# Seven products for keys and a quarter of the queries, and a plain projection stage in source order

## The chip, the core and the metric

The kernel runs on one NeuronCore of one Trainium2 chip. The metric is the device time of one execution in microseconds; the kernel before takes 2573.16 us (median of 3 runs, 2572.2 to 2574.59). Five engines work side by side, each through its own instructions in order: TensorE (PE in the profile) multiplies, VectorE (DVE) and ScalarE (ACT) do elementwise work, GpSimd (POOL) does some of it and issues some transfers, SyncE (SP) only issues transfers; ACT issues transfers too.

## What is computed

One layer of an encoder over 768 tokens (512 of a prompt, 256 of a sample), in float32:

```python
def hybrid_layer(x, ...):
    h = rmsnorm(x, ln_mix_g)
    z = h @ w_in                      # 2048 -> 2560: fourier 1024 | q 1024 | k 256 | v 256
    of = fourier_mix(zf, w_fourier)   # per 128-channel group: Re(2-D DFT), then a linear map
    q = apply_rope(q, cos, sin)
    k = apply_rope(k, cos, sin)
    oa = window_attention(q, k, v, attn_sink)
    mixed = concatenate([rmsnorm(of, ...), rmsnorm(oa, ...)])
    x = x + mixed @ w_out
    h = rmsnorm(x, ln_mlp_g)
    u = relu(h @ w_up)                # 2048 -> 8192
    return x + (u * u) @ w_down
```

A final rmsnorm follows. In the softmax a learned number per head ("sink") stands in the denominator.

## The kernel before

**Arithmetic.** Every large product is made of three TensorE products of split operands: `split` writes a rounded part with ACT ("high", `wh`) and the remainder with DVE ("low", `wl`), and high*high, high*low and low*high are added in PSUM. A TensorE instruction here multiplies a 128x128 block of weights by 384 tokens (half of them, `HALF`) or by 512 columns.

**Seven products.** Where 2x2 blocks allow it, eight block products are replaced by seven (Winograd's form of Strassen's scheme): the four blocks of weights and of tokens are added and subtracted, and the seven results are added. The MLP uses it throughout (lines 1229 and 1664), and so does the Fourier quarter of `w_in`.

**Order of the first stages.** (1) Until 41 us: the tokens are loaded, scaled and split, and `v` is computed. (2) The seven-product stage for the 1024 Fourier columns: `names7` names the products in order (a11, s1, s2, s3, a22, s4, a12). `cols7` does not exist yet: the columns come in 2 groups `g` of two 256-column blocks, and each product has 2 halves `e` of the sum, so there are 4 steps to a product and `NP7` = 28 steps. Step `n` calls, in this order: `sum7(n+3)` (DVE adds weight blocks), `high7(n+3)` (ACT), `low7(n+2)` (DVE), the token sums and splits that are due (`high_at` on ACT, `low_at` on DVE), `product7(n)` (24 TensorE instructions), `out7(n-1)` (copies a result from PSUM by ACT, or adds it to an earlier one by DVE; finished results are stored by ACT's queue), `load7(n+5)` (SP). SP, ACT, DVE and PE take these in source order. The norms of the rows are taken on the way: `row_load` (POOL's queue) and `row_square` (ACT) in four rounds at steps 10 to 18, then `row_norms` (DVE and POOL), `row_turn` (a transpose on PE after step 21) and `row_spread`.
(3) The plain stage: 20 pieces (5 blocks of 256 columns: k and four of q; 4 pieces to a block, 48 TensorE instructions each, line 835). `piece_split(p+2)` splits the weights two pieces ahead and calls `piece_load(p+4)`. Between the halves of the pieces stands the Fourier work of eight groups (`fold`, `stage1`, `stage2`; `after(t, fn)` puts `fn` behind piece `t`, where x.5 is the middle), and from piece 10 on the rotation of k and of three blocks of q (`cross` on POOL, `turned` on DVE, `parts` on ACT and DVE, stores by ACT's queue). Here only PE is in source order (SP for the first loads, and all engines from piece 19 on); for the others a planner chooses the order.
(4) Attention and the output projection, by a list of due times (`at`, `later`); the last block of q is rotated there. (5) The MLP.

PSUM has eight banks. In the seven-product stage before, four carry the tag `f` and four the tag `ps`; results of s1 and s4 get banks of their own (`Y`).

## Time and profile before

| what | value |
|---|---|
| median of 3 runs | 2573.16 us |
| the profiled execution | 2573.4 us, its span 2571.6 us |
| granted TensorE clock | 0.999 |
| MLP, share of the chain that ended last | line 1229 36%, line 1664 35% |
| output projection, the same (line 1082) | 10% |
| plain stage, the same (line 835) | 5% |
| seven products of `w_in`, the same (line 277) | 5% |

The share of a line in the chain is the part of the span in which the work that ended last went through that line. Time is taken off by shortening a stage only if its own bound is shortened: where PE is always busy, PE instructions.

### The profile page before, as it was taken

Reading aid. Unit: us, or ns where it says so; the run is one execution under the profiler, and the core shown is the slowest. Engines: PE = TensorE matmul, PEld = TensorE weight load, DVE = VectorE, ACT = ScalarE, POOL = GpSimd, SP = SyncE. Lnnn points to the kernel's source line nnn. Section 1 sums busy time; section 2 is a strip of 40 time slices with the busy share of each in tenths; the row PEclk is TensorE's granted clock in tenths of the full one; section 3 lists DMA queues with packets and bytes.
Section 4 is the critical chain, followed back from the end, with each engine's and each line's share of the span. In section 5 each row is a group of like instructions: output and inputs, shape, how many; then the busy total and the mean of one; then the engine's idle time right before and its main releaser. Section 6 shows DMA issues by size and latency. Waiting matters only on the chain.

```text
span 2571.6 us, 34801 instructions
## 1 busy us (share of the span) xinstructions
PE 2561.1 (100%) x13463; PEld 2345.3 (91%) x13463; DVE 1793.4 (70%) x2221; ACT 1121.7 (44%) x1622; POOL 242.9 (9%) x345
## 2 busy tenths in 40 slices
PE   9999999999999999999999999999999999999998
PEld 9999998888899999999999999988888888888887
DVE  8966468786465565656777777667766766777687
ACT  7644337674233333334445444433333333333335
POOL 0102322223201001100000000100000000000000
PEclk9999999999999999999999999999999999999999
DMA  8753567455655454456666666775543662554364
GB/s 305 234 182 122 178 186 207 142 165 191 222 178 181 154 174 168 164 190 239 218 227 230 213 217 214 266 285 176 175 154 121 216 227 85 175 185 158 101 210 153
DMA packets 259671, 487.84 MB, mean 190 GB/s; under 512 B 20586, under 2 KB 147056, under 8 KB 259248
## 3 DMA queue, kind: packets, MB, share of 16 engines
q1 hardware_dynamic: 187968, 321.77, 39.4%
q10 hardware_dynamic: 58512, 112.05, 11.5%
q0 software_dynamic: 13024, 51.79, 6.1%
q8 instruction: 106, 1.74, 0.3%
q14 instruction: 61, 0.50, 0.1%
HBM read 365.99 MB, written 119.54 MB: 189 GB/s over the span
## 4 chain that ended last, share of the span: by engine, by line
PE 97%; DVE 1%; DMA 1%; issue 0%; POOL 0%; SPq 0%; ACT 0%; POOLq 0%; DVEq 0%; ACTq 0%
PE pu L1229 36%; PE pd L1664 35%; PE pm L1082 10%; PE pz L835 5%; PE p L277 5%; PE pv L447 1%; PE o L960 1%; PE s L881 1%; PE t L938 1%; PE pe L664 0%; PE pa L643 0%; PE ptx L137 0%; DVE zs L729 0%; DMA raw<-in_w_out 0%; POOL zy L720 0%
## 5 line engine op out<-in xcount | busy, mean ns | idle before, releaser
L1229 PE MATMUL pu<-xf,wh 128*128 128x384 f32 x3072 | 780.2, 334 | 0.0
L1229 PEld LDWEIGHTS pu<-xf,wh 128*128 128x128 f32 x3072 | 554.2, 188 | 1.5 <-ACT o L1247 1.3
L1664 PE MATMUL pd<-wh,sh 128*128 128x512 f32 x1332 | 517.7, 389 | 0.0
L1664 PE MATMUL pd<-wl,sh 128*128 128x512 f32 x1332 | 517.7, 389 | 0.0
L1664 PE MATMUL pd<-wh,sl 128*128 128x512 f32 x1332 | 517.5, 389 | 0.0
L1229 PE MATMUL pu<-xf,wl 128*128 128x384 f32 x1536 | 513.1, 334 | 0.0
L1641 ACT ACTIVATE wh<-rd 128x1024 fp32r<-128x1024 f32 x200 | 202.3, 1054 | 522.3 <-PE pd L1664 422.0
L1651 DVE TENSOR_TENSOR wl<-rd,wh 128x1024 fp32r<-128x1024 f32 x200 | 236.0, 1221 | 226.4 <-ACT wh L1641 225.6
L1209 ACT ACTIVATE wh<-ur 128x1024 fp32r<-128x1024 f32 x160 | 170.1, 1063 | 382.6 <-PE pu L1229 207.9
L1664 PEld LDWEIGHTS pd<-wl,sh 128*128 128x128 f32 x1332 | 250.0, 188 | 51.9
L1664 PEld LDWEIGHTS pd<-wh,sl 128*128 128x128 f32 x1332 | 249.9, 188 | 52.0 <-DVE sl L1652 0.3
L1664 PEld LDWEIGHTS pd<-wh,sh 128*128 128x128 f32 x1332 | 250.0, 188 | 51.7
L1229 PEld LDWEIGHTS pu<-xf,wl 128*128 128x128 f32 x1536 | 288.3, 188 | 0.0
L1215 DVE TENSOR_TENSOR wl<-ur,wh 128x1024 fp32r<-128x1024 f32 x160 | 195.4, 1221 | 76.1 <-ACT wh L1209 76.1
L1250 DVE TENSOR_TENSOR o<-pu,o 128x768 f32<-128x768 f32 x160 | 152.8, 956 | 122.5 <-PE pu L1229 114.9
L1634 DVE TENSOR_TENSOR rd<-rd 128x1024 f32<-128x1024 f32 x112 | 131.7, 1217 | 0.0
L1229 PE MATMUL pu<-xs,wh 128*128 128x384 f32 x512 | 129.8, 334 | 0.0
L1209 ACT ACTIVATE wh<-sx 128x1024 fp32r<-128x1024 f32 x64 | 67.9, 1062 | 130.5 <-PE pu L1229 104.3
L277 PE MATMUL p<-xs,wh 128*128 128x384 f32 x448 | 113.7, 334 | 0.0
L1652 DVE TENSOR_TENSOR sl<-sr,sh 128x768 fp32r<-128x768 f32 x111 | 105.5, 951 | 0.0
L1215 DVE TENSOR_TENSOR wl<-sx,wh 128x1024 fp32r<-128x1024 f32 x64 | 78.2, 1222 | 23.8 <-ACT wh L1209 23.6
L1229 PEld LDWEIGHTS pu<-xs,wh 128*128 128x128 f32 x512 | 92.5, 188 | 0.0
(295 smaller groups left out, 3843.2 us busy)
## 6 DMA issues: line engine op xcount, KB each, us to landing
rd<-in_w_down SPq DMA_DIRECT2D x176, 512.0 KB, 5.2
ur<-in_w_up SPq DMA_DIRECT2D x128, 512.0 KB, 3.9
sr<-sd SPq DMA_DIRECT2D x95, 384.0 KB, 5.4
pd<-o ACTq DMA_DIRECT2D x60, 384.0 KB, 2.3
o<-pd POOLq DMA_DIRECT2D x60, 384.0 KB, 6.0
sd<-sm ACTq DMA_DIRECT2D x60, 384.0 KB, 2.8
raw<-in_w_in SPq DMA_DIRECT2D x39, 512.0 KB, 4.2
raw<-in_w_out SPq DMA_DIRECT2D x32, 512.0 KB, 4.7
```

The lines of the kernel that those rows point to most:

```text
L277: nc.tensor.matmul(ps7[bank, g, r][:, :HALF], l[:, i, r * P : (r + 1) * P], x[:, o, 4 * e + i, :], start=(opens and e == 0 and i == 0 and ...
L835: nc.tensor.matmul(ps[c][s][:, :HALF], w[:, i, cs], whole[j // 2][s][o][:, 4 * (j % 2) + i, :], start=first and n == 0, stop=stop and n == 2,)
L1082: nc.tensor.matmul(ps, l(k), w[:, k % 2, :], start=(k == 0 and n == 0), stop=(k == 7 and n == 2))
L1209: nc.scalar.activation(wh[:], raw[:], AF.Copy)
L1215: nc.vector.tensor_tensor(out=wl[:], in0=raw[:], in1=f32(wh[:]), op=ALU.subtract)
L1229: nc.tensor.matmul(ps[:, t, :HALF], w[:, i, t * P : (t + 1) * P], xb[:, o, i, :], start=(s == first_of[bank] and i == 0 and n == 0), stop= ...
L1250: nc.vector.tensor_tensor(out=o, in0=src, in1=o, op=ALU.add)
L1634: add = lambda x, y, op: nc.vector.tensor_tensor(out=x[:], in0=x[:], in1=y[:], op=op)
L1641: nc.scalar.activation(wh[:], t[:], AF.Copy)
L1651: nc.vector.tensor_tensor(out=wl[:], in0=t[:], in1=f32(wh[:]), op=ALU.subtract)
L1652: nc.vector.tensor_tensor(out=sl[:], in0=sr[:], in1=f32(sh[:]), op=ALU.subtract)
L1664: nc.tensor.matmul(o, l[:, q, ts], w[:, ns], start=(j == j0 and (q, t) == (0, 0)), stop=(j == j1 and (q, t) == (1, 2)),)
```

## The change

1. `cols7` adds a third group to the seven-product stage: block 6 (q columns 512 to 767 of q) and block 8 (k). 42 steps instead of 28. The plain stage keeps 12 pieces (q columns 0 to 255, 256 to 511 and 768 to 1023) instead of 20.
2. The PSUM banks of that stage are laid out anew (`pp0`): six banks `x` that every group keeps for the sums over a11, s2, s3 and a22, and two banks `t` for s1, s4 and a12, one for each row block `r`. The groups use these two in turn. `product7` finishes row block 0 before it begins row block 1, and `out7(n, 0)` empties block 0 in step `n`, `out7(n, 1)` block 1 in step `n+1`. The result of a11 is stored to DRAM and loaded again (`back7`) for the last sum.
3. The order in a step: `product7(n)`, `out7(n-1, 1)`, `low7(n+2)`, `out7(n, 0)`, `sum7(n+3)`, `high7(n+3)`, `high_at`, `low_at`, `k_at`, stores, `load7(n+5)`. The token steps are laid at other numbers, the row norms at steps 16 to 28.
4. k is rotated in steps 29 to 43 of that stage; the scaled tables of the rotation are stored and loaded again.
5. The plain stage is in source order on all engines from its first instruction; the Fourier groups begin one piece earlier and the rotations are laid at pieces 1 to 10.
6. In the softmax the sign of the queries and of the mask is turned, so that a minimum takes the place of a maximum and one small DVE instruction per head goes. The part of SBUF that is kept for the descriptors of POOL's transfers is 4096 instead of the default number of bytes.

```diff
+        pp = pctx.enter_context(tc.tile_pool(name="pp0", bufs=1, space=PSUM, reuse_waits="tile"))
-        NP7 = 4 * len(names7)
+        cols7 = ((0, 1), (2, 3), (6, 8))
+        NS7 = 2 * len(cols7)
+        NP7 = NS7 * len(names7)
...
         def product7(n):
+            name, g, e = of7(n)
+            own = name in ("s1", "s4", "a12")
+            opens = own or name == "a11"
             wh, wl = w7.pop(n)
-            x = xs[w % 2]
-            for i in range(4):
-                for r in range(2):
+            x = xs[n // NS7 % 2]
+            for r in range(2):
+                if e == 0 and opens:
+                    ps7[own, g, r] = pp.tile([P, 512], F32, tag="t" if own else "x", bufs=2 if own else 6, name="p7")
+                for i in range(4):
                     for q, (l, o) in enumerate(((wh, 0), (wh, 1), (wl, 0))):
...
+            elif s == "s4":
+                z, put = c7.pop((0, g, r)), (0, 1)
+                add(z, z)
+            else:
+                z, put = c7.pop((2, g, r)), (0, 0)
+                add(z, z)
+            if put:
+                c, t = put
+                dst = home7(g, c, r)[:, t * HALF : (t + 1) * HALF]
+                put7.append(lambda: nc.scalar.dma_start(dst, z[:]))
...
+            step(low_at, 12 + 2 * e, lambda e=e: difference(e))
+            step(high_at, 13 + 2 * e, lambda e=e: xhigh(h1, fx["d"], e))
+            step(low_at, 13 + 2 * e, lambda e=e: xlow(l1, fx["d"], h1, e))
+            step(low_at, 16 + e, lambda e=e: xsum(b11, b21, b11, e))
+            step(high_at, 18 + e, lambda e=e: xhigh(h0, b11, e))
+            step(low_at, 19 + e, lambda e=e: xlow(l0, b11, h0, e))
...
+            for s, n in enumerate((36, 38, 40)):
+                step(k_at, n - 1, lambda s=s: k_cross(s))
+                step(k_at, n, lambda s=s: k_turn(s))
+                step(k_at, n, lambda s=s, n=n: k_parts(s, n))
...
             for n in range(NP7):
+                product7(n)
+                out7(n - 1, 1)
+                low7(n + 2)
+                out7(n, 0)
+                sum7(n + 3)
+                high7(n + 3)
                 for fn in high_at.get(n, ()):
                     fn()
-                sum7(n + 3)
-                high7(n + 3)
-                low7(n + 2)
                 for fn in low_at.get(n, ()):
                     fn()
-                product7(n)
-                out7(n - 1)
+                for fn in k_at.get(n, ()):
+                    fn()
+                stores7(1 if n % 2 else 0)
                 load7(n + 5)
...
-                if n == 18:
+                if n == 24:
                     row_norms()
-                if n == 21:
+                if n == 26:
                     row_turn()
...
-            out7(NP7 - 1)
-            out7(-1)
+            out7(NP7 - 1, 1)
+            stores7()
+            for n in range(NP7, NP7 + 2):
+                for fn in k_at.get(n, ()):
+                    fn()
...
-        n_in = 4 * len(cols)
+        n_in = 4 * (len(cols) - 2)
...
-        with tc.manual_schedule(engines={mybir.EngineType.SP}):
-            piece_load(0)
-            piece_load(1)
+        last = ExitStack()
+        last.enter_context(tc.manual_schedule(engines={SP, Activation, DVE, Pool}))
+        piece_load(0)
+        nc.sync.dma_start(cc[:], a["c_chan"])
...
+        piece_load(1)
+        load_group(0)
+        open_rotation()
+        load_z(1)
+        load_group(1)
         piece_split(0)
         piece_split(1)
```

More of the change, by code (lines that the diff above doesn't have):

```diff
@@ new lines, in parts_of @@
+        def parts_of(z, hi, out, scale, s, when=lambda dt, fn: fn(), dts=(0, 0)):
+            ts = slice(s * 256, (s + 1) * 256)
+            put = lambda o, x: nc.scalar.dma_start(out[o][:, ts].rearrange("(b p) t -> p b t", p=P), x)
+            if scale is None:
+                nc.scalar.activation(hi, z, AF.Copy)
+                low = lambda: nc.vector.tensor_tensor(out=z.bitcast(F32R), in0=z, in1=f32(hi), op=ALU.subtract)
+            else:
+                nc.scalar.activation(hi, z, AF.Copy, scale=scale)
+                low = lambda: nc.vector.scalar_tensor_tensor(
+                    out=z.bitcast(F32R), in0=z, scalar=scale, in1=f32(hi), op0=ALU.mult, op1=ALU.subtract
+                )
+            put(0, f32(hi))
+            when(dts[0], low)
+            when(dts[1], lambda: put(1, z))
```

371 lines of the change are left out of this document (204 added, 167 removed).

## The prediction

> **What bounds the kernel now.** First the page: its busy shares and the engines along the chain that ended last.
>
> ```profile
> span 2571.6 us, 34801 instructions
> PE 2561.1 (100%) x13463; PEld 2345.3 (91%) x13463; DVE 1793.4 (70%) x2221; ACT 1121.7 (44%) x1622; POOL 242.9 (9%) x345
> PEclk9999999999999999999999999999999999999999
> PE 97%; DVE 1%; DMA 1%; issue 0%; POOL 0%; SPq 0%; ACT 0%; POOLq 0%; DVEq 0%; ACTq 0%
> ```
>
> PE is the bound nearly everywhere. The busy share of PE alone isn't enough, since its ends are modelled, so I next take the busy time by stage, and the chain piece by piece.
>
> ```profile
> core 0: us, PE busy (x) PEld busy (x) DVE busy (x) ACT busy (x) POOL busy (x), PEclk, DMA share, GB/s
> 0.00:41.00 41.00, 39.76 (x307) 38.90 (x308) 34.42 (x55) 35.11 (x64) 0.19 (x4) 1.00 0.94 352
> 41.00:98.00 57.00, 57.00 (x331) 57.00 (x330) 52.18 (x42) 35.55 (x48) 3.43 (x6) 1.00 0.65 217
> 98.00:157.60 59.60, 59.60 (x346) 59.51 (x345) 42.22 (x45) 35.40 (x52) 8.13 (x12) 1.00 0.68 223
> 157.60:200.00 42.40, 42.40 (x267) 42.40 (x266) 26.71 (x57) 18.01 (x46) 1.46 (x1) 1.00 0.51 163
> 200.00:286.00 86.00, 86.00 (x578) 85.80 (x576) 44.44 (x104) 38.68 (x96) 23.21 (x14) 1.00 0.37 117
> 286.00:361.30 75.30, 75.30 (x438) 75.30 (x438) 42.48 (x60) 20.78 (x32) 24.74 (x25) 1.00 0.61 207
> 361.30:450.00 88.70, 87.85 (x454) 73.73 (x453) 73.99 (x220) 64.17 (x149) 19.94 (x34) 1.00 0.72 206
> ```
>
> ```profile
> 41.05 91.53 PE p L277 x528
> ...
> 170.58 8.32 PE pz L835 x48
> ...
> 193.30 4.17 PE pz L835 x24
> 198.16 4.18 PE pz L835 x24
> ...
> 206.10 4.17 PE pz L835 x24
> ```
>
> From 41 to 361 us PE and its weight loads have no gap. One instruction costs 91.53/528 = 0.1734 us in the seven-product stage and 8.32/48 = 0.1733 us in the plain one; a step of 24 is 4.16 us. A plain piece with its Fourier group repeats after 206.10 - 193.30 = 12.80 us. DVE is the second engine: 52.18 of 57.00 us in the first half of the seven products.
>
> **What is saved.** The seven-product stage grows from 28 to 42 steps, 14 x 24 = 336 instructions more; the plain stage loses 8 pieces of 48, 384. The difference is 48 instructions x 0.1734 = 8.3 us, at the bound, with no idle time of PE behind which it could vanish. The Fourier matmuls stay. The DVE instructions dropped from the softmax lie in a stage where PE has 88.70 - 87.85 = 0.85 us of idle time, so I put them at 0 (at best -0.9). [...] All else depends on whether the new order keeps PE fed; there are three places.
>
> **Place 1: the two-engine chain in the seven products.** Durations, from starts of back-to-back instructions:
>
> ```profile
> 44.49 1.05 ACT L254 ACTIVATE wh<-wr 128x1024 fp32r<-128x1024 f32 x1
> 45.44 1.47 ACT L311 ACTIVATE xs<-xr 128x1536 fp32r<-128x1536 f32 x1
> 88.62 1.21 DVE L262 TENSOR_TENSOR wl<-wr,wh 128x1024 fp32r<-128x1024 f32 x1
> 89.75 1.75 DVE L308 TENSOR_TENSOR xr<-xr,xr 128x1536 f32<-128x1536 f32 x1
> 91.42 1.21 DVE L246 TENSOR_TENSOR wr<-wr,raw 128x1024 f32<-128x1024 f32 x1
> 101.79 1.01 DVE L294 TENSOR_TENSOR z<-p,z 128x384 f32<-128x384 f32 x2
> 102.72 1.21 DVE L262 TENSOR_TENSOR wl<-raw,wh 128x1024 fp32r<-128x1024 f32 x1
> ```
>
> On DVE a weight low or sum takes 89.75 - 88.62 = 1.13, a token sum or low 1.67, an add from PSUM (102.72 - 101.79)/2 = 0.47. Steps 14 to 17 and 19 to 20 each hold low, sum, token work and add: 1.13 + 1.13 + 1.67 + 0.47 = 4.40 against 4.16 of PE. In steps 13 and 15 the new order adds a wait. DVE's add of block 0 waits for PE's middle of the step (2.08), then comes the weight sum, then ACT's weight high (1.05) and only behind it ACT's token high (1.47), then DVE's token low: DVE stands still for 2.5 us. From the middle of step 13 to the low of step 18 DVE's chain is 0.47 + 1.13 + 1.05 + 1.47 + 1.67 = 5.8 (step 13), 4.4 (14), 1.13 + 5.8 (15), 0.47 + 1.13 (16) and some 0.3 of hand-overs, 19.0: done 21.1 us after step 13 began, where PE reads it at 5 x 4.16 + 0.2 = 21.0. The low of step 20 comes 2 x 4.40 = 8.8 us later, PE 8.3: about **0.7 us** of PE (0 to 1.5).
>
> The row norms come on top. Their loads share the token tile that step 15 still uses, so they start late.
>
> ```profile
> 95.69 0.54 POOL L517 DMA_DIRECT2D d<-in_x_prompt  x1 [6.01 <-ACT d L521]
> 102.64 0.64 ACT L521 ACTIVATE d<-d 128x512 f32<-128x512 f32 x1 [2.37 <-DMA d<-in_x_prompt]
> 121.50 0.18 DVE L524 TENSOR_REDUCE ss<-ssx 128x6 f32<-128x24 f32 x1 [0.99 <-ACT d L521]
> 122.95 2.21 POOL L101 TENSOR_TENSOR r<-r,mhalf 128x6 f32<-128x6 f32 x1
> ```
>
> A round is 102.64 - 95.69 = 7.0 us from issue to square. ACT reaches the first squares 33.6 us after step 13 began: they stand behind the weight high of step 21 and a token high (1.05 + 1.47), and these behind DVE's sum for step 21, which ends at 21.1 + 8.8 + 1.13 = 31.0. Three further rounds, the last squares (2), reduce and power (122.95 + 2.21 - 121.50 = 3.7) end near 60; PE asks for the transpose behind step 26, at 14 x 4.16 + 0.7 = 59.0. So PE waits 0 to 2, I take **1.0**. DVE itself stands behind the reduce, which waits for ACT, which waits for a DMA; it enters s4 about a step late.
>
> There the two `t` banks decide: PE may open step 32 only when DVE's add of step 31's block 0 is done. On time, that add has 2.08 us of slack; a full step late, PE waits about 2. Between 0 and 2.5 I take **1.0**. Sum of place 1: 2.7 (0 to 6).
>
> **Place 2: the boundary to the plain stage.** Before, the planner put the splits of pieces 0 and 1 ahead of the last results:
>
> ```profile
> 146.67 1.22 DVE L70 TENSOR_TENSOR wl<-raw,wh 128x1024 fp32r<-128x1024 f32 x1
> 155.36 0.85 ACTq L302 DMA_DIRECT2D zf<-z  x2
> 158.76 1.01 DVE L294 TENSOR_TENSOR z<-p,z 128x384 f32<-128x384 f32 x2
> ```
>
> The low of piece 0 ran 11 us before PE needed it, and the last add (158.76) even after the plain stage had begun. In source order the add of step 41's block 1 comes first and waits for the last matmul; ACT's queue then holds the store of that result, which waits for the add, and one store of k, and only then the high of piece 0; its low follows on DVE. PE's loss from its last seven-product matmul: add 0.55, two issues on ACT 0.85, high 1.05, hand-overs and the weight load about 0.4: 2.85; four matmuls (0.7) run while the low (1.22) is made, 0.5 more: **3.3 us** (2.0 if an issue costs ACT nothing, 4.2 if the lag of place 1 still stands). Nothing covers it: all that PE could do stands behind piece 0.
>
> **Place 3: SP's queue behind the boundary.** `load_z(1)` waits until the last store has landed, and the loads of piece 2 stand behind it.
>
> ```profile
> raw<-in_w_in SPq DMA_DIRECT2D x39, 512.0 KB, 4.2
> zf<-z ACTq DMA_DIRECT2D x16, 192.0 KB, 4.6
> zs<-zs SPq DMA_DIRECT2D x2, 768.0 KB, 6.2
> ```
>
> The store, issued 0.7 us behind the boundary, lands at 3.0 to 5.3; then 768 + 64 + 384 + 512 KB at the 352 GB/s of the first window are 4.9 us, with some 1.5 of latency: piece 2's weights are there at 9.7 to 11.7. In source order ACT and DVE must split them (1.05 + 1.22) before the first Fourier group, which before took this long from its first instruction to its low part:
>
> ```profile
> 170.50 0.96 DVE L596 TENSOR_TENSOR zf<-zf,rb 128x768 f32<-128x768 f32 x1 [6.30 <-DMA zf<-zf]
> ...
> 175.11 0.96 DVE L70 TENSOR_TENSOR sl<-fs,sh 128x768 fp32r<-128x768 f32 x1
> ```
>
> That is 5.6 us, some 5 without a weight low that lay between. PE wants the low part in the middle of piece 1, 3.3 + 8.3 + 4.2 and two small groups of matmuls (1.3) = 17.1 us behind the boundary. It is in time if the weights land by 17.1 - 2.3 - 5 = 9.8: a loss of 0 to 2, I take **0.5**. After that the plain stage has room: DVE was busy for 26.71 + 44.44 + 42.48 = 113.6 us there; without the rotation of k (3 x 2.7, rival B) and 8 lows (9) some 96 are left for 12 x 8.3 + 37 = 137 us of PE.
>
> **Sum.** -8.3 + 2.7 + 3.3 + 0.5 = -1.8. The profiled execution took 2573.4 us (its span 2571.6), 0.2 above the median; 2573.4 - 1.8 = 2571.6, on the scale of the median **2571.4 us**. The measurement tells about 0.2%, 5.1 us, from no change; the forecast is within it.
>
> **Rival A, the full gain.** Places 1 and 3 come out at 0 and the boundary is short, because the splits of piece 0 aren't held by the last store (then the plain stage isn't in source order there, and the change doesn't do what it says). Time: 2573.2 - 8.3 = 2564.9; with 3.3 at the boundary alone it is 2568.2, already within 0.2%. For it: DVE's mean load in the longer seven-product stage falls, since the token work is the same over 42 steps instead of 28. Against it: the order of the diff. Chance 0.28.
>
> **Rival B, the bank hand-over decides.** The two `t` banks change hands by a DVE add at n = 32, 34, 36, 38 and 40. If DVE is over 2.08 us late again at the last four too, PE loses 2 at each: 2571.4 + 8 = 2579.4, slower. What could make it late stands there: the k rotation, on DVE beside POOL.
>
> ```profile
> L720 POOL TENSOR_TENSOR zy<-zs,sinr 128x256 f32<-128x256 f32 x24 | 22.4, 961 | 33.4 <-ACT zs L848 22.3 <-DVE zs L729 9.9 <-DMA zs<-zs 1.2
> L729 DVE TENSOR_TENSOR zs<-zs,zy 128x256 f32<-128x256 f32 x24 | 11.3, 508 | 0.0
> L727 DVE TENSOR_TENSOR zs<-zs,cosr 128x512 f32<-128x512 f32 x12 | 10.3, 859 | 8.0 <-POOL zy L720 8.0
> L70 DVE TENSOR_TENSOR tabl<-tab,tabh 128x512 fp32r<-128x512 f32 x2 | 1.4, 690 | 0.4 <-ACT tabh L69 0.4
> ```
>
> With POOL at work 512 elements take DVE 859 ns, without it 690. Six POOL multiplies of 0.96 stand in steps 35 to 39, so at worst DVE loses 5.8 us. Against it: two steps hold 8.3 us, and their DVE work, two lows, two adds, one turn (0.86 + 2 x 0.51) and one low of that length, 2.7 for a rotation, is some 6. Chance 0.17.
>
> [...]
>
> **Rival C, the clock falls.** A gap of 3 us has no example in the stages here: the granted clock is 1.00 in every window, with no idle over 1 us inside. If half the clock came with the gap at the boundary and lasted as long, PE would lose half of 3.3 more: 2573.0, still no change. Chance 0.09. [...]
>
> **Range and chances.** Forecast 0.46, A 0.28, B 0.17, C 0.09. Faster by over 0.2% is A: 0.28; within it the forecast and C: 0.55; slower B: 0.17. The likeliest case by itself spans 2568 to 2577 (place 1 at 0, or at 6 with the boundary at 4.2). The range goes from A with part of the idle 0.85 us gained too, 2564.3, to B, 2579.
>
> **What would show it.** In the new profile: line 277's successor x1008 and the plain products x576; gaps of PE around steps 18 to 20, ahead of the transpose, at step 32 and, the largest, of some 3 us between the two stages, ended by the high and the low of piece 0. If PE runs without a gap there, place 2 is wrong and A holds. If each hand-over in s4 and a12 shows a wait for a DVE add, B holds. A slice with a lower PEclk shows C. The forecast is wrong in its ground if the plain stage itself shows gaps once per Fourier group.

## The result and the profile after

The changed kernel takes 2597.1 us (median of 4 runs, 2596.11 to 2598.05), the kernel before beside it 2573.25 (4 runs). The ratio is 1.0092, its 95% interval 1.0075 to 1.011: 24 us slower, above the range of the prediction (2564.3 to 2579). The profiled execution has a span of 2596.3 us.

From its page, to be held against the rows of before:

```profile
PE 2562.4 (99%) x13415; PEld 2344.4 (90%) x13415; DVE 1811.3 (70%) x2152; ACT 1127.1 (43%) x1622; POOL 242.6 (9%) x345
PE 90%; DVE 4%; DMA 2%; ACT 2%; issue 1%; POOL 0%; SPq 0%; ACTq 0%; DVEq 0%; POOLq 0%
```

PE has 13463 - 13415 = 48 instructions less, as counted, but only 90% of the chain that ended last runs through it, not 97%. The busy time by stage shows where it stood still (PE, then weight loads, then the clock as the last but two):

```profile
core 0: us, PE busy (x) PEld busy (x) DVE busy (x) ACT busy (x) POOL busy (x), PEclk, DMA share, GB/s
41.40:98.00 56.60, 56.60 (x329) 56.60 (x328) 41.08 (x35) 28.97 (x37) 0.00 (x0) 1.00 0.74 254
98.00:140.00 42.00, 41.67 (x238) 40.88 (x237) 34.48 (x33) 18.18 (x25) 4.59 (x9) 1.00 0.62 197
140.00:182.00 42.00, 38.06 (x210) 37.45 (x209) 27.18 (x24) 24.55 (x35) 5.58 (x9) 0.96 0.73 257
182.00:226.50 44.50, 44.50 (x250) 44.50 (x249) 33.33 (x45) 15.50 (x20) 7.50 (x7) 0.97 0.75 249
226.50:250.00 23.50, 14.68 (x82) 14.05 (x81) 10.14 (x18) 6.26 (x13) 1.41 (x2) 0.85 0.67 226
250.00:356.00 106.00, 101.64 (x659) 100.88 (x659) 71.29 (x157) 50.14 (x131) 29.17 (x23) 0.98 0.32 106
356.00:381.00 25.00, 24.15 (x147) 23.62 (x145) 15.36 (x22) 8.00 (x12) 10.29 (x9) 1.00 0.76 246
381.00:400.00 19.00, 13.97 (x59) 11.52 (x60) 13.81 (x35) 9.44 (x20) 3.22 (x4) 0.82 0.88 245
```

Before, nothing was missing up to 361 us. Now no stage but the first half of the seven products and its end is whole, and in five windows the clock is below 1.00. What PE waited for (us in total, times, the longest):

```profile
PE pa L750 <- ACT sh L69: 8.4, 1, 8.4
PE pm L1198 <- ACT ofh L1181: 5.1, 1, 5.1
PE pa L761 <- DVE cw L70: 4.3, 4, 1.3
PE p L287 <- DVE z L301: 2.0, 1, 2.0
PE pr L625 <- POOL r L101: 1.9, 1, 1.9
PE s L999 <- ACT zs L968: 0.8, 1, 0.8
```

In the code these are: the first Fourier group (`stage1` reads the high part `sh`), the first rows of the output projection (`split_of`), the fifth PSUM tile of each Fourier group (`cw` is the weight of `weights(g)`), the add that frees bank `t` in step 32, the row transpose, and the first scores.

To compare kernels, one more number is worked out from the trace: the time from each weight load of PE to the next, less 0.1734 us, summed where it comes to more than 0.12 us, between 41 and 400 us. What falls into a stretch of half clock and is the longer duration of its instructions (in the first stretch of the changed kernel 0.320 us from load to load; counted up to 0.1734 more for each) is a column of its own. "Behind" is the first 27 us of the plain stage, "groups" its rest, "attention" what comes behind its last instruction.

| us of PE lost | seven products | behind | groups | attention | half clock | sum | span |
|---|---|---|---|---|---|---|---|
| before | 0.0 | 0.0 | 0.2 | 2.1 | 0.0 | 2.3 | 2571.6 |
| after | 5.7 | 9.4 | 5.2 | 6.6 | 6.1 | 33.0 | 2596.3 |

33.0 - 2.3 - 8.3 saved = 22.4 of the 24.7 us between the spans; 2.3 stays unassigned. "The boundary" below is the first instruction of the plain stage.

### The profile page after: what moved, and what is told of

Its sections match the earlier page's. It is cut to its first block, busy times and chain, and to the rows that moved or that the text cites. A ratio compares the mean times of both kernels' runs of the same rounds, so it can differ in the third digit from the quotient of the medians.

```text
span 2596.3 us, 34652 instructions
## 1 busy us (share of the span) xinstructions
PE 2562.4 (99%) x13415; PEld 2344.4 (90%) x13415; DVE 1811.3 (70%) x2152; ACT 1127.1 (43%) x1622; POOL 242.6 (9%) x345
## 3 DMA queue, kind: packets, MB, share of 16 engines
q10 hardware_dynamic: 60240, 114.01, 11.7%
## 4 chain that ended last, share of the span: by engine, by line
PE 90%; DVE 4%; DMA 2%; ACT 2%; issue 1%; POOL 0%; SPq 0%; ACTq 0%; DVEq 0%; POOLq 0%
PE pu L1345 36%; PE pd L1780 35%; PE pm L1198 9%; PE p L287 4%; PE pv L543 1%; PE pz L959 1%; PE o L1076 1%; PE s L999 1%; PE t L1054 1%; DVE wl L273 0%; PE ptx L138 0%; DMA qh<-zh 0%; DVE wr L257 0%; ACT wh L69 0%; DMA ofr<-ofd 0%
## 5 line engine op out<-in xcount | busy, mean ns | idle before, releaser
L287 PE MATMUL p<-xs,wh 128*128 128x384 f32 x672 | 173.1, 338 | 2.0 <-DVE z L301 2.0
L287 PEld LDWEIGHTS p<-xs,wh 128*128 128x128 f32 x672 | 123.2, 191 | 2.3 <-ACT xs L407 2.3
L287 PE MATMUL p<-xs,wl 128*128 128x384 f32 x336 | 114.0, 339 | 0.3 <-DVE wl L273 0.2
```

What stands on the lines that cost most here:

```text
L287: nc.tensor.matmul(ps7[own, g, r][:, :HALF], l[:, i, r * P : (r + 1) * P], x[:, o, 4 * e + i, :], start=(opens and e == 0 and i == 0 and q ...
```

## The experiments

The theory: each loss has a cause of its own, an order in one engine's queue, and can be taken out alone. The rival: the shorter stage lacks throughput (transfers or DVE), and a wait taken out returns elsewhere. All kernels are the changed one with the edit shown; times are medians, ratios stand against the kernel before on the same chip, and "less" or "more" against 2597.1. The losses:

| run | seven | behind | groups | attention | half clock | sum | span |
|---|---|---|---|---|---|---|---|
| e3 | 0.8 | 9.8 | 5.3 | 6.6 | 2.2 | 24.7 | 2587.6 |
| e1 | 7.0 | 3.4 | 5.8 | 6.5 | 3.7 | 26.3 | 2588.2 |
| e5 | 8.0 | 6.1 | 5.6 | 6.5 | 5.1 | 31.3 | 2593.5 |
| e9 | 6.5 | 5.9 | 5.3 | 6.6 | 4.8 | 29.1 | 2592.0 |
| e14 | 8.0 | 1.2 | 8.9 | 6.3 | 4.9 | 29.3 | 2591.5 |
| e4 | 6.9 | 7.6 | 2.0 | 8.0 | 6.6 | 31.1 | 2593.3 |
| e2 | 5.9 | 9.2 | 5.2 | 4.7 | 6.8 | 31.7 | 2594.7 |
| e6 | 6.3 | 9.9 | 5.3 | 7.3 | 4.4 | 33.3 | 2596.0 |
| e10_turns | 5.7 | 10.1 | 7.3 | 6.6 | 7.3 | 37.0 | 2600.4 |
| e10_turns_at9 | 7.0 | 9.1 | 7.2 | 7.2 | 6.0 | 36.6 | 2599.5 |
| e13 | 8.4 | 9.1 | 5.2 | 4.8 | 5.5 | 33.0 | 2595.9 |
| e8 | 8.6 | 3.1 | 10.0 | 0.5 | 6.9 | 29.1 | 2593.3 |
| e7 | 1.7 | 7.0 | 2.4 | 10.0 | 3.5 | 24.6 | 2587.0 |
| e11 | 3.8 | 4.5 | 7.1 | 5.3 | 5.2 | 26.0 | 2588.6 |
| e12 | 0.3 | 1.0 | 4.2 | 7.0 | 2.6 | 15.0 | 2576.2 |
| e17 | 1.4 | 1.1 | 9.3 | 5.4 | 4.1 | 21.4 | 2582.3 |

Span less sum lies between 2560.9 and 2564.2 in all of them: the table accounts for the differences to some 3 us. Each row is of one execution, so its span is not the median. Stages that an edit does not touch move by 1 to 3 us from run to run (the seven products between 5.7 and 8.6), so a difference below that says little.

### Place 1: the order on ACT in the seven products (e3)

```diff
+                for fn in high_at.get(n, ()):
+                    fn()
                 sum7(n + 3)
                 high7(n + 3)
-                for fn in high_at.get(n, ()):
-                    fn()
```

> Edit: in the seven products ACT takes the token high of a step ahead of the weight high of three steps later, as the kernel before did. Theory (place 1 of the prediction: DVE stands still for 2.5 us in steps 13 and 15 because of this order, and the lag lasts to step 32): DVE's two waits of 2.58 us shrink below 1.5, the three gaps at 116 to 134 (1.2 us together) go, those at the transpose and at step 32 (2.3 each, with 3.4 us of half clock behind each) go or fall below 1 us; 3 to 8.7 us less than the changed kernel (2588 to 2594). Rival (DVE's sum of work is the limit there, not the order): only the 1.2 us go.

Measured: 2589.68 us, ratio 1.0066 (1.0051 to 1.0081), 7.4 less. The timeline of the changed kernel, ACT and DVE at step 13 (in brackets the idle time before, and what ended it):

```profile
98.11 1.21 DVE L257 TENSOR_TENSOR ws<-ws,wr 128x1024 f32<-128x1024 f32 x1
...
99.44 1.06 ACT L265 ACTIVATE wh<-ws 128x1024 fp32r<-128x1024 f32 x1 [5.13 <-DVE ws L257]
100.40 1.47 ACT L407 ACTIVATE xs<-d 128x1536 fp32r<-128x1536 f32 x1
...
101.91 1.76 DVE L410 TENSOR_TENSOR xs<-d,xs 128x1536 fp32r<-128x1536 f32 x1 [2.58 <-ACT xs L407]
```

DVE's sum, ACT's weight high, ACT's token high, DVE's token low: a chain across two engines in which DVE stands still for 2.58 us, though ACT had been idle for 5.13. The same places with the old order:

```profile
94.64 1.49 ACT L407 ACTIVATE xs<-d 128x1536 fp32r<-128x1536 f32 x1 [0.54 <-DVE d L404]
...
97.90 1.22 DVE L257 TENSOR_TENSOR ws<-ws,wr 128x1024 f32<-128x1024 f32 x1
99.03 1.75 DVE L410 TENSOR_TENSOR xs<-d,xs 128x1536 fp32r<-128x1536 f32 x1
```

The wait is gone, and with it the gaps at steps 18 to 22, the wait ahead of the transpose and most of that at step 32 (2.0 us fall to 0.6): 5.7 us fall to 0.8, and the half clock behind them goes. It was the order, not DVE's sum of work.

### Place 3: the first Fourier group (e1, e5, e9, e14)

SP's queue behind the boundary (PE's first plain instruction is at 224.66), and what follows on ACT:

```profile
222.68 0.33 SPq L79 DMA_DIRECT2D raw<-in_w_in  x1
223.10 0.37 SPq L695 DMA_DIRECT2D wf<-in_w_fourier  x1
228.43 0.33 SPq L697 DMA_DIRECT2D zf<-zf  x1
229.71 0.33 SPq L813 DMA_DIRECT2D cosr<-cosd  x1
230.09 0.43 SPq L813 DMA_DIRECT2D sinr<-sind  x1
230.62 0.37 SPq L834 DMA_DIRECT2D zs<-zs  x1
...
233.76 0.86 SPq L79 DMA_DIRECT2D raw<-in_w_in  x2
...
240.19 1.06 ACT L69 ACTIVATE wh<-raw 128x1024 fp32r<-128x1024 f32 x1 [9.81 <-DMA raw<-in_w_in]
...
245.80 0.84 ACT L69 ACTIVATE sh<-fs 128x768 fp32r<-128x768 f32 x1 [0.89 <-DVE fs L721]
```

The weights of piece 2 are asked for at 233.76 and are there at 240.19, 15.5 us behind the boundary; the first group stands behind them in ACT's and DVE's queue. Two orders lie on top of each other: SP's, and that of the splits. e1 puts the load of piece 2 ahead on SP:

```diff
         piece_load(1)
+        piece_split(0)
         load_group(0)
...
         load_group(1)
-        piece_split(0)
         piece_split(1)
```

> Edit: the split of piece 0, and with it the load of piece 2's weights, stands in the source ahead of the loads of the first Fourier group, of the rotation tables and of pair 1, so SP issues it before it waits for the last store. Theory (each gap of PE has its own cause in the order of a queue): the gap of 8.6 us at 237.9 and the one of 0.8 at 246.7 go, with the 1.5 us lost at half clock behind them; 8 to 11 us less than the changed kernel (2586 to 2589), all other gaps as they are. Rival (transfers and engines are the limit behind the boundary): pair 1 and the second group now land later, the wait moves to another load, and less than 4 us are gained.

Measured: 2590.94 us, ratio 1.007 (1.0055 to 1.0085), 6.2 less. The loss falls from 9.4 to 3.4, short of the expectation by the row of the waits that takes its place:

```profile
PE pc L711 <- DMA wf<-in_w_fourier: 3.1, 1, 3.1
```

`wf` is an input and depends on nothing here, yet SP stood 6.1 us ahead of its issue, until a store of ACT's queue had landed. The trace's records of the changed kernel, with the completion semaphore that each transfer signals and waits for, tell why:

```
223.37  ACT  store zs<-z   signals 109
225.45  ACT  store zs<-z   signals 99
223.10  SP   load wf       waits for 108, signals 108
228.38  SP   wait for 109
228.43  SP   load zf       signals 109
229.65  SP   wait for 101 and 99
229.71  SP   load cosr     signals 99
```

In this trace the 1133 transfers of SP and ACT signal eight semaphores (99, 101, 104 to 109), 141 or 142 times each, as in turn, and 1001 of them have a wait for their own one ahead of them, that is for the transfer eight places earlier in the turn. The store issued at 223.37 landed at 228.37, and SP's wait for 109 ended at 228.40; 99 and 101 were signalled at 228.97 and 229.64, and SP's wait for the two ended at 229.68. So here a load on SP stands behind a store in ACT's queue that itself waits for a DVE add, without sharing data with it. e5 takes the last six stores out of that turn (POOL's 169 transfers signal semaphores of their own, 110 to 117):

```diff
-                put7.append(lambda: nc.scalar.dma_start(dst, z[:]))
+                put7.append(lambda: (nc.gpsimd if n >= 36 else nc.scalar).dma_start(dst, z[:]))
```

> Edit: only the six stores of the last block of the seven products go out on POOL's DMA queue instead of ACT's. Background: in the trace each transfer of SP and ACT signals one of eight completion semaphores in turn, and waits until the transfer eight places earlier in the program has landed; the load of the first Fourier group stands eight places behind the first store of the last pair, so it would wait for that store although it reads nothing of it. Theory (shared semaphores): with these stores out of the turn, SP issues the tables, piece 1 and the first Fourier group 5 us earlier or more, PE's waits of 8.6 and 0.8 us at 237.9 fall below 2 in all and the half clock behind them goes; 8 to 11 us less than the changed kernel (2586 to 2589). Rival (the data or its memory is what SP waits for, or the transfers lack throughput): the wait for the last store stays and less than 3 us are gained.

Measured: 2593.35 us, ratio 1.0078 (1.0063 to 1.0093), 3.7 less. SP's load of `zf`:

```profile
222.51 0.33 SPq L697 DMA_DIRECT2D zf<-zf  x1
```

It is issued 5.9 us earlier, 2 ahead of the boundary: the semaphores were what held it. But the loss falls only to 6.1, because `raw` of piece 2 still goes out behind some 2.4 MB of other loads (at 229.68) and the fold still stands behind it. e9 moves that order: for piece 0, `piece_split(2)` comes behind `weights(0)` and `fold(0)`; e14 puts it behind `fold_parts(0)` too, at the end of the piece (its diff is shown).

```diff
-            piece_split(piece + 2)
+            if piece:
+                piece_split(piece + 2)
...
             for fn in todo.pop(piece, ()):
                 fn()
+            if not piece:
+                piece_split(2)
```

> Edit: only for piece 0, the folded weights and the fold of the first Fourier group stand ahead of the split of piece 2 in the source, so ACT and DVE no longer hold them behind weights that land 15.5 us after the boundary. Theory (the wait of 8.4 us is that order on ACT and DVE; the group's own rows land some 4 us after their issue at 228.4, its fold takes 4): the high part is there at about 237, PE's gaps at 237.9 and 246.7 fall from 9.4 us to 1 or less and the half clock goes; 9 to 11 us less than the changed kernel (2586 to 2588). Rival (the weights of piece 2 are the limit): PE runs into the same wait at piece 2, 4 to 5 us later, and 4 or less are gained.

> Edit: only for piece 0, fold, high and low part of the first Fourier group all ahead of the split of piece 2. Theory (the wait of 8.4 us is that order on ACT and DVE): the gaps at 237.9 and 246.7 fall from 9.4 us to 1.5 or less together, no half clock there; 8.5 to 10.5 less than the changed kernel (2586.5 to 2588.5). Rival (piece 2's weights are the limit): as much is lost at the begin of piece 2.

Measured: 2593.38 us (ratio 1.0074, 1.0059 to 1.0089) and 2593.31 (1.0078, 1.0064 to 1.0091). In e9 the high part `sh` still stood behind the split, and the loss fell to 5.9 only; the expectation had overlooked this. In e14 it is 1.2, as expected, but the next group loses what was gained:

```profile
PE pa L761 <- DVE cw L70: 7.9, 4, 4.6
```

The 4.6 us are the fifth PSUM tile of the second group: the bank it wants is free once DVE has made the low part `cw`, and that stands behind the low part of the group before, a rotation and a weight split, all of them late. Alone, then, the rival is partly right here. With the next edit beside it (e12 below) the loss behind the boundary is 1.0; but the same tile of the second group then waits 2.3 us, for ACT's copy of a Fourier result, and 3.4 us at half clock follow.

### The Fourier groups (e4)

In every group five tiles of tag `f` follow one another within a microsecond or two, with four banks. The folded weights half a piece earlier keep the first and the fifth apart:

```diff
-                after(g - 0.5, lambda g=g: (weights(g), fold(g)))
+                after(g - 0.5, lambda g=g: (g == 0 and weights(0), fold(g)))
...
                 after(g, lambda g=g: fold_parts(g))
+            if g + 1 < FG:
+                after(g, lambda g=g: weights(g + 1))
```

> Edit: the folded weights of Fourier group g+1 are computed half a piece earlier, behind the last stage-1 matmuls of group g-1, so that the fifth PSUM tile of a group no longer follows its first one closely. Theory (four banks of tag f; the fifth tile waits until DVE has made the low part of the first): the gaps of 1.1 to 1.4 us once per group at 263, 290, 304, 317, 331 go, 4 to 5.5 us less than the changed kernel (2592 to 2593). Rival (DVE is full in the plain stage): PE waits for DVE at another tile of the same group, and less than 2 us are gained.

Measured: 2594.65 us, ratio 1.0083 (1.0066 to 1.01), 2.5 less. The groups fall from 5.2 to 2.0 us, the wait for `cw` is gone, and a new one of 1.1 us (for ACT's copy of a Fourier result, which stands behind the small copies of the next fold) takes part of it back. `weights(1)` now came before its `wf` had landed (3.4 us of waits for it), so from here on only groups 2 to 7 are moved.

### The start of the attention (e2, e6, e10, e13)

The high part of the first Fourier rows waits for a load behind the loads of q on SP. e2 puts the load ahead of them; e6 puts both behind the load of k:

```diff
+        after(9, lambda: load_q(0))
+        after(9, lambda: load_of(0, [...]))
         after(9.5, fourier_norm)
-        after(9.5, lambda: load_q(0))
         after(9.5, lambda: load_q(2))
-        after(10, lambda: load_of(0, [...]))
```

> Edit: the load of the first Fourier rows for the output projection stands in SP's order ahead of the first load of q instead of behind two of them. Theory: its data was ready near 368, so it lands before PE asks for it; the gap of 5.3 us at 380.6 goes and the half clock behind it, 5 to 8 us less than the changed kernel (2589 to 2592). Rival (at the start of the attention the loads of q are needed just as early): the loss moves to the first scores or the first softmax rows and 0 to 2 us are gained.

> Edit: the loads of the first unit of q and of the first Fourier rows stand right behind the load of k, half a piece to a piece earlier in the source, so that fewer stores of the last rotated pair stand within eight places ahead of them. Theory: both now land before PE asks; of the 6.4 us of gaps at 379 to 386 and the 1.6 at half clock behind them less than 2 us are left; 5 to 8 less than the changed kernel (2589 to 2592). Rival (the data comes late itself: the rotated rows or the Fourier rows are stored too late): the gain is below 2, as when the Fourier rows alone were moved.

Measured: 2596.97 (ratio 1.0092, 1.0077 to 1.0107) and 2598.54 (1.0099, 1.0082 to 1.0116): no gain. In e2 PE waits for q instead:

```profile
PE s L999 <- DMA qs<-ql: 2.8, 1, 2.8
PE pm L1198 <- ACT ofh L1181: 1.4, 1, 1.4
```

In e6 the rows were loaded 8 us earlier and had landed by 377, but ACT's queue held their high part until 386.02, behind a weight split and the last store of pair 3, which waits for a low part on DVE: there the order on ACT was the limit. So the rotation was moved a piece ahead, alone and with the loads of e6:

```diff
-        turns = [...] + [(2, s, t) for s, t in enumerate((7, 8, 8.5))] + [(3, s, t) for s, t in enumerate((9, 9.5, 10))]
+        turns = [...] + [(2, s, t) for s, t in enumerate((6, 7, 7.5))] + [(3, s, t) for s, t in enumerate((8, 8.5, 9))]
```

> Edit: the rotation of pairs 2 and 3 a piece earlier; the order of the loads as in the changed kernel. Background: with only the loads earlier (the two runs before) PE's wait of 5 to 6 us at 380 stayed, since ACT's queue held the high part of the first Fourier rows behind the last store of pair 3, which waits for a low part on DVE behind the splits of the output weights. Theory (two causes that end at the same time: the loads behind the stores of q, and ACT's queue behind the rotation): the rotation alone lets the stores and so the loads come a piece earlier too; of the 8.5 us lost there less than 3 remain, 5 to 8 less than the changed kernel (2589 to 2592). Rival (the splits of the output weights hold ACT): less than 2 gained.

> Edit: rotation of pairs 2 and 3 a piece earlier and the loads of the first unit of q and of the first Fourier rows right behind the load of k. Theory: 6 to 8.5 us less than the changed kernel (2588.5 to 2591), at most 1.5 us of gaps left at the start of the attention. Rival (the splits of the output weights hold ACT): less than 2 gained.

Measured: 2602.39 (ratio 1.0107, 1.009 to 1.0124) and 2602.8 (1.0111, 1.0096 to 1.0127), 5 to 6 us more. The loss at the attention stays at 6.6 and 7.2, and at the last groups, where the rotation now stands, `cw` is late by 3.2 us. e13 tries the transfers instead: k in three parts, the first 384 KB ahead, the rest behind the Fourier rows and q.

```diff
+            load_k(0, 1)
...
+        after(9, lambda: load_of(0, [...]))
+        after(9, lambda: load_q(0))
+        after(9.5, lambda: load_k(1, 1))
...
+        after(10.5, lambda: load_k(2, 2))
```

> Edit: only the loads at the start of the attention: k in three parts, the first 384 KB, then the first Fourier rows and the first q, the rest of k later. Theory (the single transfer of 1.5 MB, landing after 9.2 us, holds up the stores and loads behind it, among them the output weights whose split stands ahead of the Fourier rows in ACT's queue): the wait of 5 us for the high part falls below 2 and the half clock there goes, 5 to 8 less than the changed kernel (2589 to 2592). Rival (all these transfers together, 8.8 MB in 35 us, are the limit, in whatever order): less than 2 gained, the wait moves to q or k.

Measured: 2597.5 us, ratio 1.0091 (1.0075 to 1.0106). The loss there is 4.8 instead of 6.6; the total does not move.

### The plain stage in the planner's order (e8)

Contents and source as changed; between SP's first loads and the last piece only PE is in source order.

> Edit: the plain stage keeps its contents and its source, but only SP's prologue and the last piece are in source order; in between the planner orders the engines, as in the kernel before. Theory (source order on all engines is not itself the cause; two of the three losses of the plain stage come from the order of transfers, the third from four PSUM banks): the gap at 237.9 stays, since SP's prologue stays, the one-per-group gaps shrink; 2590 to 2597. Rival (the hand-made order on ACT, DVE and POOL is the cause of most of it): the plain stage loses less than 8 us in all, 2580 or less.

Measured: 2593.92 us, ratio 1.008 (1.0065 to 1.0095), 3.2 less. The theory gave the time (2590 to 2597) but not the way: the planner takes away 6.3 us behind the boundary and nearly all at the attention, against what was expected, and loses 10.0 in the groups, where stage 2 now waits for low parts. So the order by hand is not the whole cause: of 21.2 us lost in the plain stage and at the attention 13.6 stay with the planner's order, at other places, and the half clock too.

### Together (e7, e11, e12, e15 to e17)

e7 joins e3, e4 (groups 2 to 7), e5, e6 and the row transpose a step later; e11 joins e3, e4 (the same), e9, e10_turns_at9, the transpose and two token lows a step later; e12 joins e3, e4 (the same), e14 and e13.

> Edit: all together: token high first in the seven products, the row transpose one step later, the last six stores on POOL's queue, the folded weights of groups 2 to 7 half a piece earlier, and the loads of q and of the first Fourier rows behind the load of k. Theory (separate causes, each in the order of a queue): the losses of 33.7 us between 41 and 400 us fall to 5 or less; 2563.5 plus 0 to 6: 2564 to 2570, faster than the kernel before. Rival (the shorter plain stage lacks throughput): the gaps reappear at other tiles and the time stays above 2576.

> Edit: all of these: token high first in the seven products, the row transpose a step later, the token lows of steps 30 and 32 a step later (behind the add that frees the bank), the first fold ahead of the split of piece 2, the folded weights of groups 2 to 7 half a piece earlier, the rotation a piece earlier with its loads behind the load of k. Theory (separate causes, each an order in a queue): 33.7 us of losses between 41 and 400 us fall to 5 or less; 2564 to 2569, faster than the kernel before. Rival (a limit of throughput): new gaps, above 2576.

> Edit: four single edits together: token high first in the seven products; for the first Fourier group fold, high and low part ahead of the split of piece 2; the folded weights of groups 2 to 7 half a piece earlier; k loaded in three parts (384, 384, 768 KB), the first Fourier rows and the first q right behind the first part. Theory (separate causes that add up): left are 0.8 us in the seven products, 1 behind the boundary, 2.5 in the groups, 1 to 3 at the attention: 5 to 7.5 of 33.7, so 2568.5 to 2571.5, under the kernel before. Rival (transfers at the attention and behind the boundary are the limit): 8 us or more stay, 2576 or above.

Measured: e7 2588.67 us (ratio 1.0058, 1.0043 to 1.0073), e11 2590.07 (1.0061, 1.0046 to 1.0076), e12 2580.5 (1.0027, 1.0018 to 1.0036): 16.6 us less than the changed kernel and still slower than before. All three lie where the rival put them (2576 or above), not where the theory did: the losses do not add up as single ones. In e7 and e11 the order of the first group's splits still costs 6.1 and 3.1 us (`sh`). What PE waits for in e12, whose profiled execution took 2578.01 us:

```profile
PE pm L1205 <- ACT ofh L1188: 3.8, 1, 3.8
PE pa L761 <- ACT of L784: 3.2, 2, 2.3
PE s L1006 <- ACT zs L973: 2.7, 1, 2.7
```

Of the first list the wait for `sh`, that for the transpose and that for bank `t` are gone; 7.0 of the 15.0 us left are the attention. e15 and e16 put the results of a group ahead of the next fold, e15 with the rotation a piece earlier. In both, the squares of a Fourier group stand ahead of the fold that still needs the rows they overwrite, so the Fourier part computes something else and the fold waits for POOL; their times (2590.75 and 2586.22) therefore say nothing on the total. e17 adds to e12 the rotation a piece earlier and puts the third piece of the output weights ahead of the Fourier rows on SP.

> Edit: the four edits of the combined run before, the rotation of pairs 2 and 3 a piece earlier, and in each half piece the results of the group before (stage 2, stage 1) ahead of the fold of the next. Theory (the rest is order on ACT: the last copy behind pair 2's store, the Fourier rows behind pair 3's last store): at the attention 2 us or less are left of 7, at the group 0.5 of 2.6, no half clock; 2565 to 2570, under the kernel before. Rival (the transfers at the attention are the limit): 5 us or more stay there, 2573 or above.

> Edit: as the run beside it, but the rotation as in the changed kernel. Theory: the gap at the group goes (2 us less than the four edits together, with its half clock 3.5), the 7 us at the attention and their half clock stay: 2575 to 2579. Rival (ACT's order at the attention is decided by the loads alone): the loss there falls below 3 here too.

> Edit: the four edits together (token high first, first fold ahead of piece 2's split, folded weights early, k in three parts), the rotation of pairs 2 and 3 a piece earlier, and the load of the third output weight piece ahead of the first Fourier rows and q on SP. Theory (order in ACT's queue): of the 7 us of gaps at the attention in the run of four edits 2.5 or less are left; the groups keep 4 us; 2572 to 2577. Rival (the transfers are the limit at the attention): 5 us or more of gaps stay there with the half clock behind them, 2578 or above.

Measured for e17: 2584.24 us, ratio 1.0044 (1.0031 to 1.0058), 3.7 more than e12. At the attention 5.4 us stay, by the rival's bound; the waits are spread over q, the Fourier rows and the output weights. What makes e17 slower than e12 lies elsewhere: the groups lose 9.3 us instead of 4.2, where 4 were expected. Beside the earlier rotation the fifth tile waits for ACT's copy in four groups:

```profile
PE pa L761 <- ACT of L784: 6.6, 4, 2.3
```

The windows of 15 us at the attention, for the kernel before:

```profile
345.00:360.00 15.00, 15.00 (x88) 15.00 (x88) 6.76 (x10) 5.40 (x9) 0.00 (x0) 1.00 0.85 267
```

for the changed kernel, whose plain stage ends at 379:

```profile
345.00:360.00 15.00, 15.00 (x99) 15.00 (x99) 10.07 (x16) 6.10 (x12) 8.01 (x7) 1.00 0.36 125
360.00:375.00 15.00, 15.00 (x93) 15.00 (x92) 9.33 (x14) 3.89 (x5) 6.86 (x7) 1.00 0.79 268
375.00:390.00 15.00, 9.12 (x40) 7.88 (x39) 8.43 (x15) 5.12 (x8) 5.30 (x7) 0.77 0.97 273
```

for e17 (plain stage until 367):

```profile
360.00:375.00 15.00, 12.92 (x63) 11.67 (x62) 6.63 (x11) 4.37 (x7) 5.09 (x5) 0.89 1.04 255
```

and for e8, in the planner's order (until 384):

```profile
375.00:390.00 15.00, 14.73 (x83) 13.76 (x82) 7.43 (x12) 5.96 (x11) 3.72 (x4) 1.00 0.90 258
```

The last but one column is the share of the transfer engines. Before, they were at 0.85 in the 15 us ahead of the end of the plain stage (361), and k had been asked for at 313. In the changed kernel k, q, the Fourier rows and three pieces of output weights all go out from 358 on, since the tiles of k and q lie in memory that the Fourier stage gives up behind piece 9 of 12; the share is 0.36 up to 360 and 0.97 where PE already waits, in e17 1.04. In e2, e10_turns and e17 one wait gave way to another, which would fit transfers as the limit. Three things on record speak against that as the whole cause. In e6 the Fourier rows lay ready for 9 us. In the changed kernel SP stood for 9.0 us, until 371.43, on a load of output weights that waits for a low part on DVE; the first loads of q stood behind it, and from 370 to 375 the share was 0.48. And in e8 the same tiles are loaded from 360.86 on, 23 us ahead of the end of the plain stage (in the changed kernel 21), and only 0.5 us is lost: there the first loads of q went out right behind k, at 362.19, and from 355 to 390 three stores of rotated q were left instead of eleven. So memory that comes free late does not make the loss by itself. Whether the 2 to 3 us more, the fewer stores or the order on SP made the difference, no run separates: the limit at the attention stays open.

## Why the prediction was wrong

Term by term, foreseen and measured (less what the kernel before loses): place 1 2.7 and 5.7 us, place 2 3.3 and 0, place 3 0.5 and 9.4; and, put at nothing, the later groups 5.0, the attention 4.5 and the half clock 6.1. Together that is 24.2 us more than foreseen, and 2571.4 + 24.2 = 2595.6 against 2597.1 measured. The steps that failed are place 3 and the sentence on the room in the plain stage.

**What is saved** was right in its count, 48 instructions. Of the 8.3 us 6.0 are seen: the span less the losses is 2569.3 before and 2563.3 after.

**Place 1** was right in its mechanism. The 2.58 us of DVE, the gaps at steps 18 to 22, the wait ahead of the transpose and the one hand-over at step 32 are all there, and e3 shows that the order on ACT makes them. The size was off: 5.7 us instead of 2.7, inside the bounds (0 to 6), and then half clock behind two of the gaps, which the sum did not hold.

**Place 2** was wrong. PE goes from the last seven-product instruction into the plain stage without a gap. ACT's and DVE's rows for piece 0:

```profile
212.21 1.06 ACT L69 ACTIVATE wh<-raw 128x1024 fp32r<-128x1024 f32 x1 [1.07 <-PE p L287]
...
215.54 1.21 DVE L70 TENSOR_TENSOR wl<-raw,wh 128x1024 fp32r<-128x1024 f32 x1
```

The split stands 12 us ahead of the boundary, in front of stores that come earlier in the source: that a later stage stands behind an earlier one in the queue held for piece 1, not for piece 0. So the plain stage was not in source order on ACT and DVE from its first instruction; what put piece 0 ahead, no run shows.

**Place 3** was the failing term: 0.5 us foreseen, 9.4 measured and half clock behind it. PE's demand was right (17.1 - 3.3 = 13.8 us behind the boundary without the stall of place 2; measured 237.9 - 224.5 = 13.4), and so was the work on the first group (2.3 + 5; from 240.19 to the end of the low part at some 247.6 it is 7.4). The weights were foreseen at 9.7 to 11.7 us (the terms given add up to 9.4 to 11.7), and came at 15.5. No run shows the 1.5 us of latency among the terms; the runs show whole times from issue to landing, 4.2 us in the median of the 512 KB loads of `w_in` before and 6.35 for this one, issued at 233.76 and landed at 240.11. The landing of the last store was foreseen well (3.0 to 5.3 us; SP goes on at 229.65, 5.0 behind the boundary), but the bytes behind it were not: the first group's rows and the two rotation tables, 3 x 384 KB, were left out of the count, since nothing in them needs that store; the shared semaphores held them back too. At the 352 GB/s of the prediction they are 3.3 us, and piece 3's weights were asked for at the same time. The price also hung on place 2: its stall would have hidden 3.3 us. e14 and e12 show that the order of the splits decides it: 1.2 and 1.0 us are left here, though part of the loss comes back in the second group.

**"After that the plain stage has room"** was wrong twice. Mean load said nothing on a hand-over: four banks and five tiles cost most of the 5.2 us in the groups (2.0 are left in e4). And the loads at the attention were not looked at; 6.6 us are lost there, by a cause that stays open.

**The rivals.** A fails: the boundary was short, yet nothing of the gain came. B fails: only step 32 waits, not 34 to 40, and most of it goes by e3. Its price was also misread. The 859 ns of the rotation before are a mean of two kinds: without a whole multiply of POOL beside it an instruction takes 0.68 to 0.69 us, with one 1.21:

```profile
291.66 1.21 DVE L727 TENSOR_TENSOR zs<-zs,cosr 128x512 f32<-128x512 f32 x1 [2.13 <-POOL zy L720]
293.50 0.69 DVE L727 TENSOR_TENSOR zs<-zs,cosr 128x512 f32<-128x512 f32 x1 [0.63 <-POOL zy L720]
```

So it costs some 0.5 us where it occurs, not 859 - 690 = 169 ns each time. Beside k's rotation in the changed kernel two weight lows of DVE took 1.51 and 1.77 us instead of 1.21, and four smaller splits 3.65 together instead of 2.20: 2.3 us in all, of the 5.8 at worst, and PE did not wait for them. C was right as a mechanism and wrong in its place and price: no gap at the boundary, but 6.1 us of half clock with four other gaps. That half clock lasts as long as its gap no run shows: stretches of 3.41, 3.41, 10.24 and 6.83 us stand with gaps of 2.25, 2.34, 8.62 and 5.31. The upper end of the range rested on one mechanism alone; that several would add up was the case left out.

## What to carry to other kernels

Where engines are put in source order, follow for each first use of a stage the whole queue in front of it, on SP, ACT and DVE, and count what the transfers in front weigh (some 2.4 MB ahead of piece 2 in e5); a mean load per engine said nothing on this here. Look for false neighbours: PSUM banks that turn within a group (the groups fell from 5.2 to 2.0 us in e4), and completion semaphores that SP's and ACT's transfers share (5.9 us on one load in e5). Moving a late load ahead gained nothing in total here in three tries (e2, e6, e13): ask first which queue or which load will be late in its place.

## What was not expected of the hardware

The price of a gap in granted clock did not go by its length here. The stretches at half clock in the changed kernel, from the trace's records of the granted clock:

```
start 157.77  length  3.41 us
start 181.66  length  3.41
start 243.10  length 10.24
start 383.05  length  6.83
```

The starts are 7, 18 and 41 times 3.413 us apart, the lengths 1, 3 and 2 times: in this execution they lie on one grid. The windows on this grid around the row transpose of the changed kernel:

```profile
154.36:157.77 3.41, 1.50 (x10) 1.18 (x9) 2.02 (x2) 3.41 (x5) 2.07 (x3) 1.00 0.71 217
157.77:161.18 3.41, 3.41 (x13) 3.41 (x12) 3.41 (x4) 1.93 (x3) 0.00 (x0) 0.50 0.98 310
```

around the longer gap at step 32 of e1:

```profile
175.24:178.65 3.41, 1.59 (x10) 1.27 (x8) 3.41 (x4) 2.73 (x4) 0.58 (x1) 1.00 0.94 331
178.65:182.06 3.41, 1.62 (x9) 1.65 (x10) 3.24 (x5) 1.38 (x2) 0.00 (x0) 1.00 0.28 95
182.06:185.48 3.42, 3.42 (x22) 3.42 (x21) 2.87 (x3) 0.93 (x2) 0.00 (x0) 1.00 0.85 255
```

and around the same gap of e8:

```profile
177.04:180.46 3.42, 1.67 (x10) 1.35 (x8) 3.42 (x3) 2.75 (x4) 0.58 (x1) 1.00 0.97 336
180.46:183.87 3.41, 1.51 (x9) 1.54 (x10) 3.35 (x5) 1.38 (x2) 0.00 (x0) 1.00 0.24 91
183.87:187.28 3.41, 3.41 (x12) 3.41 (x11) 2.75 (x3) 0.92 (x2) 0.00 (x0) 0.50 0.80 238
```

A gap of 2.25 us that left 1.18 of 3.41 us to the weight loads was followed by one window at half clock, 1.5 us of PE; a gap of 3.84 us that fell across two windows and left 1.27 and 1.65 cost nothing more. Yet in e8 a gap of 3.87 us, some 0.1 us later in its window than that of e1, left 1.35 and 1.54 us and was followed by a window at half clock. In the Fourier groups 1.77 us of idleness in a window were enough (e1), at their end 1.16 (e17, at 350), while four gaps of 1.1 to 1.4 us in the changed kernel's groups had none behind them. So neither the length of a gap nor the busy time of one window tells the price alone; what does, these runs do not show. Where the gaps fall on the grid may be why e12's ten runs spread over 6.7 us (2576.75 to 2583.41) and the kernel before, without gaps, over 1.7 in fourteen; that was not tested.

The second is the turn of eight completion semaphores above: 5.9 us on one load (issued at 228.43 in the changed kernel, at 222.51 in e5), without any data in common.
